# A decoder block's gated product and its broadcasts of 1/rms, from fp32 to fp32r in high and low parts

## The chip, the cores and the metric

The kernel runs on one core of one Trainium2 chip, in one launch. The metric is the device time of that core in microseconds. Three runs of the kernel before took 1047.62, 1047.27 and 1045.18 us; their median is 1047.27.

## The reference

One layer of a hybrid decoder block over 512 tokens of width 1024: a SwiGLU half-step, a mixer (sparse attention beside an S5 state-space layer), a second SwiGLU half-step, a gated per-layer embedding and a last RMSNorm. Everything is fp32. What the change touches is the norm and the S5 layer's gated product:

```python
def rmsnorm(x, g):
    xf = x.astype(jnp.float32)
    y = xf * lax.rsqrt(jnp.mean(xf * xf, axis=-1, keepdims=True) + RMS_EPS)
    return (y * g.astype(jnp.float32)).astype(x.dtype)

# at the end of s5_mixer: y is (1, 512, 512), w_glu is (512, 512)
    y = jax.nn.gelu(y.reshape(B, L, S5_WIDTH))
    out = y * jax.nn.sigmoid(y @ w_glu.astype(f32) + b_glu.astype(f32))

def reference(...):
    h = x
    h = h + 0.5 * swiglu(rmsnorm(h, norm_ffn1), ffn1_w1, ffn1_w3, ffn1_w2)
    z = rmsnorm(h, norm_mix) @ w_in
    ...
    h = h + jnp.concatenate([o_nsa, o_s5], axis=-1) @ w_out
    h = h + 0.5 * swiglu(rmsnorm(h, norm_ffn2), ffn2_w1, ffn2_w3, ffn2_w2)
    gate = jax.nn.sigmoid(rmsnorm(h, norm_ple) @ w_ple_gate)
    h = h + gate * (p @ w_ple)
    return rmsnorm(h, norm_final)
```

## The kernel before

**Layout.** The residual `h` stays in SBUF transposed: eight tiles of 128 features by 512 tokens. Weights come from DRAM in units of 128x1024 fp32 (512 KB), one after another on ScalarE's DMA queue, into a ring of four buffers `raw`.

**Products in three parts.** Most products use the type fp32r, and keep the precision by splitting both operands. `split` casts a unit to a high part `hi` on ScalarE (line 164) and subtracts that from the unit on VectorE to get a low part `lo` (line 166); the ring has three pairs of hi and lo. `mm3` (line 173) then issues three products, high by high, high by low and low by high, into one PSUM bank. A few products are written in plain fp32 with a single `mm`; the profile shows each of these as two records.

**Broadcasts of 1/rms.** `rsqrt_steps` (line 277) sums squares with products against a column of `ones`, takes the power -1/2 on GpSimd with one Newton step on VectorE, and has the result `ri` as 128 tokens by `nb` columns, one column for each 128 tokens. To spread it over partitions it scales the identity matrix by each column (`dg`, line 296) and multiplies `ones` (128x128) with `dg` (128x512) in one fp32 product (line 299). With `nb` = 4 this happens four times: for the first norm (`Norm.finish`, called in the first half-step), for the mixer's (`s5_input`), for the second half-step's (`norm2`, around line 1429) and for the gate's (`ng.finish`, line 1515). In the mixer and for `norm2` the broadcast is pinned to its place in TensorE's order (`pin_last`). The last norm of all uses `nb` = 2 twice.

**The mixer's order.** Attention, the S5 layer, the projections and the first half of the output product are generators; the string `PLAN` (line 1590) lists by hand in which order their steps are written: `g` is the GLU (line 1174), `s` the S5 scan, `c` the compression, `t` and `x` scores, `V` values, `p` the loads of queries, `f` half of the output product. A scheduler then orders each engine's instructions from that written order with its own model of times, except where an instruction is pinned or told to follow another (`issue_after`). The GLU's first four steps apply gelu to the four tiles `yts` (128 channels by 512 tokens). Its next four each make one block: four fp32 products of raw weights with the tiles, then tanh on ScalarE, a product on VectorE, and the split of the result into `oh` and `ol`, which the output product reads. At `close` the S5 buffers are given back and the attention's pool `ap_` takes their place, with four buffers each of the tags `eh` and `el` for the values' steps.

Of the kernel before, what the change touches and what calls it, by code (L numbers as in the profile page):

```python
# [10 lines left out]
F32 = mybir.dt.float32  # L11
FR = mybir.dt.float32r
# [3 lines left out]
OP = mybir.AluOpType  # L16
# [3 lines left out]
SEQ = 512  # L20
# [56 lines left out]
def block_kernel(ctx: ExitStack, tc: tile.TileContext, a: dict, out: bass.AP):  # L77
    nc = tc.nc
    V, S, G, PE = nc.vector, nc.scalar, nc.gpsimd, nc.tensor
    PS = bass.MemoryType.PSUM  # L80

    pers = ctx.enter_context(tc.tile_pool(name="pers", bufs=1, side="right"))
# [9 lines left out]
    def bank(tag, shape=(128, 512), dt=F32):  # L92
        return psum.tile(list(shape), dt, tag=tag, name="ps_" + tag)
# [7 lines left out]
    def load_unit(i, q, parts=None):  # L101
        w = UNIT_W[i]
        raw = ring.tile([128, UNIT], F32, tag="raw", name="raw", bufs=4)
        src = a["wpack"][128 * UNIT_OFF[i]:128 * UNIT_OFF[i + 1]]
        raws[i] = raw
        if parts is None:
            loads[i] = q.dma_start(raw[:, :w], src.rearrange("(p c) -> p c", c=w))
            return None
        src = src.rearrange("(n p c) -> n p c", p=128, n=len(parts))
        return [lambda c=c, i=i: q.dma_start(raw[:, c], src[i]) for i, c in enumerate(parts)]  # L110
# [12 lines left out]
    ident = pers.tile([128, 128], F32, name="ident")  # L123
    nc.sync.dma_start(ident, a["ident"])
    identb = pers.tile([128, 128], BF, name="identb")
    G.tensor_copy(identb, ident)
    ones = pers.tile([128, 128], F32, name="ones")
    G.memset(ones, 1.0)

    pinned = tc.keep_in_program_order  # L130

    def mm(o, lhsT, rhs, start, stop, **kw):
        return PE.matmul(o, lhsT, rhs, start=start, stop=stop, **kw)  # L133
# [10 lines left out]
    def unit(raw_only=False, keep=None, q=nc.scalar, after=None, at=None):  # L144
        i = unit_i[0] if at is None else at
        if at is None:
            unit_i[0] += 1
        w = UNIT_W[i]
        if i not in raws:
            load_unit(i, q)  # L150
        raw = raws.pop(i)
        if raw_only:
            return raw
        return split(raw, (slice(0, w),), keep, after)
# [15 lines left out]
    def split(raw, parts=(slice(0, UNIT),), keep=None, after=None, kept=free):  # L170
        return list(split_parts(raw, parts, keep, after, kept))[-1]
# [8 lines left out]
    npool = ctx.enter_context(tc.tile_pool(name="npool", bufs=1, side="right"))  # L180
# [96 lines left out]
    def rsqrt_steps(parts, nb, pin=False, pin_last=False, beside=None):  # L277
        st = bank("D", (128, 4))[:, :nb] if isinstance(parts, list) else parts
        for b in range(nb if isinstance(parts, list) else 0):
            for i, t in enumerate(parts):  # L280
                p = mm(st[:, b:b + 1], t[:, b * 128:(b + 1) * 128], ones[:, 0:1], i == 0, i == len(parts) - 1)
                if pin and b + i == 0:
                    pinned(p)
        ms, ri, t = (npool.tile([128, 4], F32, tag=n, name=n, bufs=2)[:, :nb] for n in ("ms", "ri", "nt"))
        p = V.tensor_scalar(ms, st, 1.0 / D_MODEL, 1e-6, OP.mult, OP.add)
        if beside:
            pinned(p)
        G.tensor_tensor(ri, ms, negh[:, :nb], OP.pow)
        if beside:
            beside()  # L290
        V.tensor_tensor(t, ri, ri, OP.mult)
        V.scalar_tensor_tensor(t, t, -0.5, ms, OP.mult, OP.mult)
        V.scalar_tensor_tensor(ri, t, 1.5, ri, OP.add, OP.mult)
        dg = npool.tile([128, 4, 128], F32, tag="dg", name="dg")[:, :nb]
        for b in range(nb):
            V.tensor_scalar(dg[:, b, :], ident, ri[:, b:b + 1], None, OP.mult)
        yield
        pb = bank("D")[:, :nb * 128]
        p = mm(pb, ones, dg.rearrange("p b t -> p (b t)"), True, True)
        if pin_last:  # L300
            pinned(p)
        if beside:
            pb2 = bank("C")[:, :nb * 128]
            pinned(mm(pb2, ones, dg.rearrange("p b t -> p (b t)"), True, True))
            yield pb, pb2
        yield ri, pb
# [540 lines left out]
    def mixer(ctx):  # L847
# [45 lines left out]
        at = {}  # L893
# [26 lines left out]
        def gelu2(o, x, w, tag):  # L920

            t = tp.tile([128, SEQ], F32, tag=tag, name="gt")[:, :w]
            act(t, x, AF.Square)
            V.scalar_tensor_tensor(t, t, 1 / 0.044715, x, OP.add, OP.mult)
            act(t, t, AF.Tanh, scale=math.sqrt(2 / math.pi) * 0.044715)
            V.scalar_tensor_tensor(o, t, 1.0, x, OP.add, OP.mult)
# [34 lines left out]
        for i in range(2):  # L961
            raw = tp.tile([128, SEQ], F32, tag=f"r{i + 1}", name="rope")
# [63 lines left out]
        yts = []  # L1026
# [147 lines left out]
        def glu():  # L1174
            for m in range(4):
                yt = yts[m]
                gelu2(yt, yt, SEQ, GT[m % 2])
                yield
            for m in range(4):
                if m % 2 == 0:  # L1180
                    raw = unit(True, at=next(at["glu"]))
                o = bank("A")
                for k in range(4):
                    q = (m * 4 + k) % 8
                    mm(o, raw[:, q * 128:(q + 1) * 128], yts[k], k == 0, k == 3)
                sg = mp.tile([128, SEQ], F32, tag="ra", name="sg", bufs=2)

                act(sg, o, AF.Tanh, scale=0.25, bias=bglu[:, m:m + 1])
                V.scalar_tensor_tensor(sg, sg, 1.0, yts[m], OP.add, OP.mult)
                S.activation(oh[:, 4 + m], sg, AF.Copy, scale=0.25)  # L1190
                V.scalar_tensor_tensor(ol[:, 4 + m], sg, 0.25, oh[:, 4 + m].bitcast(F32), OP.mult, OP.subtract)
                yield
# [133 lines left out]
        def values(qb, env):  # L1326
# [3 lines left out]
            for g in range(2):  # L1330
# [40 lines left out]
                for par in range(2):  # L1371
# [9 lines left out]
                    v=v_gates(), s=s5_all(), c=cmp_all(), g=glu(), f=out_half(range(4, 8)))  # L1381
# [3 lines left out]
        for step in PLAN.split():  # L1385
            if step == "close":
                s5x.close()
                ap_ = ctx.enter_context(tc.tile_pool(name="att", bufs=2, reuse_waits="tile"))
# [41 lines left out]
    for m in range(KT):  # L1430
        if m % 4 == 0:
            wu = unit()
        o = bank("B")
        for k in range(2):
            q = (m * 2 + k) % 8
            sl = slice(q * 128, (q + 1) * 128)
# [15 lines left out]
    with tc.tile_pool(name="gate", bufs=2, reuse_waits="tile") as gp:  # L1452
# [59 lines left out]
        for m in range(KT - 3):  # L1512
            o = products(m, unit(), slice(0, SEQ))
# [5 lines left out]
        for i, wu in wl.items():  # L1519
            sq = gated(i, products(i, wu, c0), c0)  # L1520
# [29 lines left out]
        sq = gated(7, os[7], c1, pinned, {"gt": ends(E[1]), "h": ends(E[2])})  # L1550
# [4 lines left out]
        pb, pb1 = rsqrt_rows(st, 2, beside=ends(KT))  # L1555
# [32 lines left out]


PLAN = """u u u k s s u k k q s q s Q p3 s s s k s Q s t3 t3 s t3 z t3 s s t3 s p3 s z t3 t3 s s t3 t3 s g t3 g t3 g t3  # L1590
v t3 c v v c t3 v c c p2 t2 t3 t3 t2 p2 c c c t2 c c t2 t2 c v t2 t2 t2 t2 t2 t2 t2 t2 t2 g close p1 p1 p0 x3
p0 g t2 g t2 g g t1 t1 x2 f S2 t1 f t1 t1 f t1 t1 f f t0 t0 R2 f x1 t0 R3 V3 V3 V3 V3 V3 V3 V3 V3 V3 V3 V3 V3
V3 V3 V3 V3 x0 f V3 t1 V3 V3 V2 V2 V2 V2 V2 t0 V2 V2 V2 V2 V2 S0 V2 R1 R0 V2 V2 V2 V2 V1 V1 V1 V1 V1 V1 V1
V1 V1 V1 V1 V0 V0 V0 V0 V0 V0 V0 f"""
# [155 lines left out]
```

## Time and profile before

| | |
|---|---|
| median of three runs | 1047.27 us (1045.18 to 1047.62) |
| the profiled execution: its own time | 1044.96 us |
| its span, first to last instruction | 1043.2 us |
| mean granted TensorE clock | 0.999 |
| TensorE products busy | 1030.2 us in 6057 instructions |
| VectorE busy | 824.5 us |
| ScalarE busy | 501.9 us |
| GpSimd busy | 159.2 us |

The profile is of one execution. Its page gives the busy time of each engine, the chain of work that ended last, and groups of instructions by line, operation and tile. PE is TensorE's products, PEld its weight loads, DVE is VectorE, ACT ScalarE, POOL GpSimd, SP SyncE. A row of the chain reads: start in us, length in us, engine, output tile, line, number of instructions. A row of the timeline reads: start, length, engine, line, operation, output from inputs, shape, count, and in brackets the idle time before it with what ended it. A row of a table by stages reads: the window, its length, then for PE, PEld, DVE, ACT and POOL the busy time and count, then clock, share of the DMA engines in use, and GB/s. Nearly all products go through the helper at line 133, so they are told apart by their tiles. An f32 in a product's form stands for fp32r as well; the tiles tell which it is.

### The profile page before, as it was taken

To read this page: it belongs to the slowest core of one execution; us is meant where nothing else is said; L and a number is where in the kernel's file an instruction comes from. 1 tells how busy PE (TensorE), PEld (TensorE's weight loads), DVE (VectorE), ACT (ScalarE), POOL (GpSimd) and SP (SyncE) were. 2 spreads that over 40 slices of the span, in tenths; PEclk is the share of its full clock that TensorE was granted. 3 is DMA by queue.
4 is the path that set the end of the run, shared out by engine and by line. 5 is a ranking of instruction groups with operands and counts; after the bars stand their busy time and mean duration, and the time that the engine had idled before them with its cause. 6 is when DMAs were issued, how large, how long until landed. Compare 5 with 4: busy or idle time off the path is not lost.

```text
span 1043.2 us, 15725 instructions
## 1 busy us (share of the span) xinstructions
PE 1030.2 (99%) x6057; PEld 875.7 (84%) x6057; DVE 824.5 (79%) x1382; ACT 501.9 (48%) x868; POOL 159.2 (15%) x180
## 2 busy tenths in 40 slices
PE   9999999999999999999999999999999999999997
PEld 6888888889889888776586688998899899899886
DVE  6798468988989766896688887996598588687666
ACT  6322232535336542476768855653365245245452
POOL 0003948207870200100000000000000000000001
PEclk9999999999999999999999999999999999999999
DMA  7434325636354748766410013433233333333412
GB/s 266 142 87 134 98 88 169 229 121 127 120 135 149 231 118 230 216 193 183 158 41 21 21 61 123 135 107 122 85 98 122 101 102 101 101 102 101 141 61 81
DMA packets 52394, 131.00 MB, mean 126 GB/s; under 512 B 10784, under 2 KB 19072, under 8 KB 52320
## 3 DMA queue, kind: packets, MB, share of 16 engines
q10 hardware_dynamic: 26352, 90.77, 27.3%
q0 software_dynamic: 5872, 17.93, 6.9%
q1 hardware_dynamic: 20096, 21.31, 6.5%
q8 instruction: 47, 0.77, 0.3%
q14 instruction: 27, 0.22, 0.1%
HBM read 114.09 MB, written 15.73 MB: 124 GB/s over the span
## 4 chain that ended last, share of the span: by engine, by line
PE 84%; DVE 5%; DMA 3%; POOL 3%; ACT 2%; issue 2%; SPq 0%; DVEq 0%; ACTq 0%; POOLq 0%
PE ps_A L133 25%; PE ps_C L133 24%; PE ps_B L133 20%; PE ps_D L133 15%; POOL ft L721 1%; POOL bt L720 1%; DMA kf<-kd 1%; DVE lo L166 1%; ACT e L918 1%; DMA kd<-r 1%; DVE el L1360 0%; DMA qf<-qd 0%; DMA h<-in_xT 0%; POOL ft L719 0%; POOL seen L559 0%
## 5 line engine op out<-in xcount | busy, mean ns | idle before, releaser
L164 ACT CAST hi<-raw 128x1024 fp32r<-128x1024 f32 (+2 forms) x143 | 144.4, 1010 | 250.3 <-PE ps_C L133 96.8
L133 PE MATMUL ps_C<-hq,hi 128*128 128x512 f32 x704 | 217.5, 390 | 0.2
L166 DVE TENSOR_TENSOR lo<-raw,hi 128x1024 fp32r<-128x1024 f32 (+2 forms) x143 | 174.2, 1219 | 40.6 <-ACT hi L164 39.9
L133 PEld LDWEIGHTS ps_C<-hq,hi 128*128 128x128 f32 x704 | 130.9, 188 | 28.1 <-DVE h L526 1.3
L133 PE MATMUL ps_C<-hq,lo 128*128 128x512 f32 x352 | 136.9, 389 | 0.0
L133 PE MATMUL ps_A<-xh,hi 128*128 128x512 f32 (+1 forms) x352 | 124.9, 355 | 0.5 <-ACT hi L164 0.5
L133 PE MATMUL ps_A<-xl,hi 128*128 128x512 f32 (+1 forms) x352 | 124.0, 352 | 0.1
L133 PE MATMUL ps_A<-xh,lo 128*128 128x512 f32 (+1 forms) x352 | 122.5, 351 | 0.2 <-DVE lo L166 0.2
L164 ACT CAST hi<-s 128x1024 fp32r<-128x1024 f32 x56 | 58.9, 1052 | 107.0 <-PE ps_D L133 60.9
L166 DVE TENSOR_TENSOR lo<-s,hi 128x1024 fp32r<-128x1024 f32 x56 | 70.7, 1262 | 19.9 <-ACT hi L164 19.7
L133 PEld LDWEIGHTS ps_C<-hq,lo 128*128 128x128 f32 x352 | 66.1, 188 | 13.8
L133 PEld LDWEIGHTS ps_A<-xh,hi 128*128 128x128 f32 x352 | 66.6, 189 | 10.2 <-ACT hi L164 0.7
L133 PEld LDWEIGHTS ps_A<-xh,lo 128*128 128x128 f32 x352 | 66.7, 189 | 9.5 <-DVE lo L166 0.6
L133 PEld LDWEIGHTS ps_A<-xl,hi 128*128 128x128 f32 x352 | 66.5, 189 | 9.7 <-DVE xl L192 0.8
L526 DVE SCALAR_TENSOR_TENSOR h<-ps_C,h 128x512 f32<-128x512 f32 x64 | 43.9, 687 | 36.6 <-PE ps_C L133 36.5
L133 PE MATMUL ps_B<-sh,lo 128*128 128x256 f32 x224 | 63.1, 282 | 0.3 <-DVE lo L166 0.3
L133 PE MATMUL ps_D<-sl,hi 128*128 128x256 f32 x224 | 63.1, 282 | 0.0
L133 PE MATMUL ps_B<-sh,hi 128*128 128x256 f32 x224 | 63.0, 281 | 0.0
L133 PE MATMUL ps_B<-sl,hi 128*128 128x256 f32 x224 | 62.9, 281 | 0.0
L133 PE MATMUL ps_D<-sh,hi 128*128 128x256 f32 x224 | 62.8, 280 | 0.0
L133 PE MATMUL ps_B<-xh,hi 128*128 128x512 f32 (+1 forms) x168 | 62.8, 374 | 0.0
L133 PE MATMUL ps_D<-sh,lo 128*128 128x256 f32 x224 | 62.6, 280 | 0.0
(440 smaller groups left out, 2474.4 us busy)
## 6 DMA issues: line engine op xcount, KB each, us to landing
raw<-in_wpack ACTq DMA_DIRECT2D x168, 512.0 KB, 3.5
si<-s5i POOLq DMA_DIRECT2D x8, 512.0 KB, 5.3
so<-s5o POOLq DMA_DIRECT2D x8, 512.0 KB, 5.6
h<-in_xT SPq DMA_DIRECT2D x8, 256.0 KB, 4.5
s5i<-fs POOLq DMA_DIRECT2D x1, 2048.0 KB, 11.5
xraw<-in_xT SPq DMA_DIRECT2D x8, 256.0 KB, 3.8
s5o<-gt POOLq DMA_DIRECT2D x1, 2048.0 KB, 13.4
s5i<-tcs POOLq DMA_DIRECT2D x2, 1024.0 KB, 10.4
```

The costliest lines, as they stand in the source:

```text
L133: return PE.matmul(o, lhsT, rhs, start=start, stop=stop, **kw)
L164: p, q = S.copy(hi[:, c], raw[:, c]), None
L166: q = V.tensor_tensor(lo[:, c], raw[:, c], hi[:, c].bitcast(F32), OP.subtract)
L526: V.scalar_tensor_tensor(h[:, m, :], o[m], 0.5, h[:, m, :], OP.mult, OP.add)
L720: G.tensor_tensor(bt, b2[:, 1], bc(psn[:, e]), OP.mult)
L721: G.tensor_tensor(ft[:, :, s_, :], ft[:, :, s_, :], bt, OP.add)
L918: S.activation(*args, **kw)
```

## The change

The kernel after does three things. The four broadcasts with `nb` = 4 are made of two fp32r products: `ri` is rounded to fp32r (`rh`), the rest `t` is taken, and both scale the identity into a `dg` of their own, the second in the buffer `sq`. The tile `ones` is declared as fp32r, and read as fp32 elsewhere. The GLU's sixteen fp32 products become `mm3`: the tiles are split into `yh` and `yl` in a new step after the four gelu steps, in the buffers `eh` and `el`, and the two weight units are split like all others. In `PLAN` one `g` is added between the two steps `p1`, for the new step.

```diff
@@ -124,7 +124,8 @@
-    ones = pers.tile([128, 128], F32, name="ones")
+    onesr = pers.tile([128, 128], FR, name="ones")
+    ones = onesr.bitcast(F32)
     G.memset(ones, 1.0)
@@ -291,6 +292,24 @@
         V.scalar_tensor_tensor(ri, t, 1.5, ri, OP.add, OP.mult)
+        if nb == 4:
+            rh = npool.tile([128, 4], FR, tag="ms", name="rh", bufs=2)
+            V.tensor_copy(rh, ri)
+            V.tensor_tensor(t, ri, rh.bitcast(F32), OP.subtract)
+            parts = []
+            for n, r in (("dg", rh.bitcast(F32)), ("sq", t)):
+                dg = npool.tile([128, 4, 128], FR, tag=n, name="dg", bufs=1)
+                for b in range(nb):
+                    V.tensor_scalar(dg[:, b, :], ident, r[:, b:b + 1], None, OP.mult)
+                parts.append(dg.rearrange("p b t -> p (b t)"))
+            yield
+            pb = bank("D")
+            for i, dg in enumerate(parts):
+                p = mm(pb, onesr, dg, not i, i == 1)
+                if pin_last:
+                    pinned(p)
+            yield ri, pb
+            return
         dg = npool.tile([128, 4, 128], F32, tag="dg", name="dg")[:, :nb]
@@ -1176,13 +1195,21 @@
                 gelu2(yt, yt, SEQ, GT[m % 2])
                 yield
+            ys = []
+            for yt in yts:
+                yh, yl = (ap_.tile([128, SEQ], FR, tag=n, name="y", bufs=4) for n in ("eh", "el"))
+                S.copy(yh, yt)
+                V.tensor_tensor(yl, yt, yh.bitcast(F32), OP.subtract)
+                ys.append((yh, yl))
+            yield
             for m in range(4):
                 if m % 2 == 0:
-                    raw = unit(True, at=next(at["glu"]))
+                    wu = unit(at=next(at["glu"]))
                 o = bank("A")
                 for k in range(4):
                     q = (m * 4 + k) % 8
-                    mm(o, raw[:, q * 128:(q + 1) * 128], yts[k], k == 0, k == 3)
+                    sl = slice(q * 128, (q + 1) * 128)
+                    mm3(o, wu[0][:, sl], wu[1][:, sl], *ys[k], k == 0, k == 3)
                 sg = mp.tile([128, SEQ], F32, tag="ra", name="sg", bufs=2)
@@ -1588,7 +1615,7 @@
-v t3 c v v c t3 v c c p2 t2 t3 t3 t2 p2 c c c t2 c c t2 t2 c v t2 t2 t2 t2 t2 t2 t2 t2 t2 g close p1 p1 p0 x3
+v t3 c v v c t3 v c c p2 t2 t3 t3 t2 p2 c c c t2 c c t2 t2 c v t2 t2 t2 t2 t2 t2 t2 t2 t2 g close p1 g p1 p0 x3
```

## The prediction

> **What bounds the kernel now.** I read the page first, then the groups of TensorE instructions with shapes kept apart, then the chain of waits around the changed places, then the timeline at each of them.
>
> ```profile
> PE 1030.2 (99%) x6057; PEld 875.7 (84%) x6057; DVE 824.5 (79%) x1382; ACT 501.9 (48%) x868; POOL 159.2 (15%) x180
> PEclk9999999999999999999999999999999999999999
> PE 84%; DVE 5%; DMA 3%; POOL 3%; ACT 2%; issue 2%; SPq 0%; DVEq 0%; ACTq 0%; POOLq 0%
> L133 PE MATMUL ps_A<-yt,raw 128*128 128x512 f32 x32 | 14.6, 599 | 0.0
> L133 PE MATMUL ps_D<-dg,ones 128*128 128x512 f32 x8 | 4.1, 592 | 0.0
> ```
>
> TensorE is busy 99% of the span at a full granted clock, and holds 84% of the chain that ended last. Time taken from its queue should therefore come off the end, unless what replaces it makes TensorE wait. The two changed groups hold 14.6 and 4.1 us. There are two records to each fp32 product: 16 GLU products give 32 records and 4 broadcasts give 8. Busy times are modelled and overlap, so I take prices from the pace of the chain:
>
> ```profile
> by line: PE ps_A L133 72.2%; PE ps_B L133 18.5%; PE ps_C L133 6.8%; PE ps_D L133 1.7%; DVE cosr L1127 0.9%; PE ps_C L1152 0.4%; PE ps_D L1322 0.3%; issue 0.1%
> 497.31 3.49 PE ps_A L133 x8
> 500.80 0.42 PE ps_B L133 x3
> 501.87 3.49 PE ps_A L133 x8
> 505.77 3.49 PE ps_A L133 x8
> 1000.24 2.72 PE ps_B L133 x12
> 36.86 0.86 PE ps_D L133 x2
> 1002.96 0.86 PE ps_D L133 x2
> ```
>
> The first row covers 483 to 546 us: around the GLU the chain is TensorE alone but for 1%. One GLU block (four fp32 products) costs 3.49 us, or 0.87 a product. The row at 1000.24 is the gate's ordinary work of twelve fp32r products, also 128x512, in 2.72 us, or 0.227 each. One fp32 broadcast costs 0.86.
>
> **The change, part by part.**
>
> GLU products on TensorE: 16 fp32 products become 48 fp32r products. A block falls from 3.49 to 12 x 0.227 = 2.72. Four blocks gain 4 x 0.77 = 3.1 us. So three passes in place of one product is a gain of a quarter only, because one fp32 product lasts as long as 3.8 fp32r ones. The Trainium skill, page FP8 and Floating Point Precision, section TensorE Precision Notes, counts four passes through the array for true FP32; with 0.227 each that is 0.91 a product and a gain of 16 x 0.227 = 3.6 us, an estimate. The row's 0.87 decides here and gives the 3.1.
>
> GLU operands: eight new splits. Their prices stand in rows of the same shapes:
>
> ```profile
> L327 ACT CAST hq<-t 128x512 fp32r<-128x512 f32 x30 | 18.7, 622 | 13.3 <-DVE t L401 13.3
> L1360 DVE TENSOR_TENSOR el<-e,eh x48: 628/692/693, 548.6 to 604.3; 128x512 fp32r<-128x512 f32 x48
> L926 DVE SCALAR_TENSOR_TENSOR yt<-gt,yt x4: 692/692/693, 448.9 to 487.1; 128x512 f32<-128x512 f32 x4
> 490.00:500.00 10.00, 10.00 (x60) 5.67 (x59) 3.55 (x9) 4.26 (x11) 0.00 (x0) 1.00 0.92 332
> 500.00:510.00 10.00, 10.00 (x38) 4.82 (x36) 7.66 (x10) 7.89 (x18) 0.00 (x0) 1.00 0.60 180
> ```
>
> The four activations need 4 x 0.62 = 2.5 us of ScalarE and 4 x 0.69 = 2.8 of VectorE. The two weight units need 2 x 1.05 = 2.1 and 2 x 1.23 = 2.5 (rows below). Together that is 4.6 on ScalarE and 5.3 on VectorE. The last of the four yt starts at 487.1 and is ready 0.69 later, at 487.8. Between 490 and 500 VectorE (third busy column) works 3.55 of 10 us and ScalarE (fourth) 4.26, so 6.4 and 5.7 us are free there: the new work fits and I cost it at nothing. If that cover is gone, because the subtractions are put ahead of older work, the price is what TensorE waits for them, up to 2.8; the second rival takes that up.
>
> The first GLU block: before, TensorE read the loaded weights directly. Now they must be cast and subtracted first, and this is the one wait that the change adds on the path.
>
> ```profile
> 492.16 0.33 ACTq L107 DMA_DIRECT2D raw<-in_wpack  x1
> 493.02 0.34 ACTq L107 DMA_DIRECT2D raw<-in_wpack  x1
> 494.66 0.33 ACTq L107 DMA_DIRECT2D raw<-in_wpack  x1
> DMA to landing us min/median/max: 3.3/4.4/5.5
> 499.09 1.04 ACT L164 CAST hi<-raw 128x1024 fp32r<-128x1024 f32 x1 [0.52 <-DMA raw<-in_wpack]
> 500.16 1.23 DVE L166 TENSOR_TENSOR lo<-raw,hi 128x1024 fp32r<-128x1024 f32 x1 [1.64 <-ACT hi L164]
> 518.51 2.98 PE ps_A L133 x15
> ```
>
> These are weight loads, the first split after them, and the first block of the output half, the next user of split weights. The load at 494.66 lands 4.4 later, at 499.06, and the cast of the first output unit starts at 499.09, having waited for it. So the loads go in order, and those at 492.16 and 493.02 are the two GLU units. The first lands near 496.6, just ahead of its block at 497.31. With the change the cast ends near 497.6 and the subtraction near 498.9. The first two products of the block need only the high part; the third needs the low one. With nothing put in between, the block is late by 498.9 - 497.3 - 2 x 0.227 = 1.2 us; with the longest landing of 5.5 it is 2.3. With enough score products put ahead of it, it is nothing. Those are there (0.42 us at 500.80, more behind the next blocks), but they need free banks. I take 0.8, nearer to the row with the median landing, with 0 and 2.3 as ends. A queue's order costs something too: behind a cast at the head of ScalarE stand the exponentials that empty the score banks, and TensorE's fillers wait for these. It is already so at 499.09, where the wait was 0.52, and it is inside the 2.3. The second unit lands near 497.8 and is split long before the third block. Two of the three hi/lo slots go to the GLU units, so the second and third output units wait for GLU blocks two and four. Block four is over well before the output half begins at 518.51, and each unit serves two of its blocks: covered. The raw slots come free earlier than before, at the subtraction, and nothing in the chain waits for these loads, so I count no gain.
>
> The broadcasts of 1/rms: four times one fp32 product (0.86) becomes two fp32r products (0.45), a gain of 0.4 each. Before them VectorE gets a cast and a subtraction of 128x4 and four more 128x128 products.
>
> ```profile
> 32.82 0.88 DVE L296 TENSOR_SCALAR dg<-ident,ri 128x128 f32<-128x128 f32 x4
> 36.70 1.02 PE L133 MATMUL ps_D<-dg,ones 128*128 128x512 f32 x2
> 376.00 0.17 DVE L293 SCALAR_TENSOR_TENSOR ri<-nt,ri 128x4 f32<-128x4 f32 x1
> 376.20 0.88 DVE L296 TENSOR_SCALAR dg<-ident,ri 128x128 f32<-128x128 f32 x4
> 377.03 1.22 DVE L166 TENSOR_TENSOR lo<-raw,hi 128x1024 fp32r<-128x1024 f32 x1
> 378.28 1.02 PE L133 MATMUL ps_D<-dg,ones 128*128 128x512 f32 x2
> 634.50 0.88 DVE L296 TENSOR_SCALAR dg<-ident,ri 128x128 f32<-128x128 f32 x4
> 635.98 1.02 PE L133 MATMUL ps_D<-dg,ones 128*128 128x512 f32 x2
> 997.42 0.87 DVE L296 TENSOR_SCALAR dg<-ident,ri 128x128 f32<-128x128 f32 x4
> 1002.80 1.02 PE L133 MATMUL ps_D<-dg,ones 128*128 128x512 f32 x2
> L296 DVE TENSOR_SCALAR dg<-ident,ri x20: 277/282/288, 32.8 to 1035.6; 128x128 f32<-128x128 f32 x20
> ```
>
> Four products of 0.28 us take 0.88, so they start 0.20 apart; a 128x4 step also starts 0.20 after the one before it (376.00 to 376.20). The low half is thus ready 0.2 + 0.2 + 4 x 0.2 = 1.2 us later than dg was.
> - First norm: 33.70 becomes 34.90, TensorE comes at 36.70. Gain 0.4.
> - Mixer's norm: 377.08 becomes 378.28. TensorE needs the high half at 378.28 and the low half at 378.51. Just in time: gain 0.4, with 0.2 us to spare. The subtraction of weights at 377.03 moves back by 1.2 to end near 379.5. The broadcast is followed by six products of its own projection (1.4 us, to 380.1 with the shorter broadcast), and only the third of the next projection reads a new low part: covered.
> - Second norm: 635.38 becomes 636.58. The high product goes at 635.98, the low one waits from 636.21 to about 636.6 and ends its slot at 636.83, where the fp32 product ended it (635.98 + 0.86 = 636.84). These products are pinned in TensorE's order, so nothing passes them. Gain 0.
> - Gate's norm: 998.29 becomes 999.49, TensorE comes at 1002.80. Gain 0.4.
>
> That is 1.2 together. The trace has no tensor_scalar that writes fp32r. From below it is no shorter than the f32 one. From above I take 0.42 us (the 128x512 cast to fp32r on VectorE at line 1356, four times as long, has that mean):
>
> ```profile
> L1356 DVE CAST eh<-e 128x512 fp32r<-128x512 f32 x14 | 5.9, 423 | 0.6 <-ACT e L918 0.5
> ```
>
> I take 0.28, since that cast pays nothing visible for its output type. At 0.42, with starts 0.34 apart, eight of them end 1.1 later still, and the two tight places lose about 1 us each: an end of +2. VectorE: DVE Perf Modes in the Trainium skill (section The DRAIN you can't avoid) speaks against such chains of short instructions: the next one starts only when the pipe has emptied. By that the extra steps last 0.17 + 0.17 + 4 x 0.28 = 1.5 instead of 1.2, an estimate that would add 0.3 us at the second norm. The row of four in 0.88 us shows starts 0.20 apart, so I keep 1.2.
>
> The moved steps: the gated product gets one more step in the written order, ahead of its products. It issues no DMA of its own. On the queues of SP and POOL nothing of the change stands. The weight loads are the same two, from ScalarE's queue.
>
> **Sum.** -3.1 (products) -1.2 (broadcasts) +0.8 (first block late) = -3.5 us. The profiled execution took 1044.96 (span 1043.2), so 1041.5. It is 2.3 under the median of the three runs, 1047.27. On the median the forecast is 1043.8. Behind the GLU comes a stretch, 546 to 606, whose chain lies on ScalarE and VectorE too; it is entered from TensorE's chain, so it starts earlier and keeps its length.
>
> **Rivals.**
>
> First, the GLU gain is largely given back at its first block: no filler, longest landing, 2.3 in place of 0.8, and wide fp32r diagonals at the mixer's norm lose 1. Net -1.0: 1043.9 for the profiled execution, 1046.3 on the median, no change. For it: the weights land only 0.7 us before their block. Against it: score products for other query blocks stand in the queue.
>
> Second, and on the other side: VectorE becomes the bound of the mixer's middle.
>
> ```profile
> 470.00:480.00 10.00, 10.00 (x77) 8.49 (x75) 6.56 (x13) 8.63 (x21) 1.17 (x2) 1.00 0.51 118
> 480.00:490.00 10.00, 8.88 (x61) 5.90 (x61) 8.70 (x17) 7.43 (x19) 0.00 (x0) 1.00 0.52 165
> 482.60 0.58 DVE L1127 TENSOR_TENSOR cosr<-cst,pe 128x256 f32<-128x256 f32 x1 [0.30 <-DMA cst<-vcd]
> ```
>
> The yt are made from 448.9 to 487.1, so the first subtractions can run as soon as their buffers are free. If they and the rest go ahead of older VectorE work, above all of the row at 482.60, for which TensorE waits, VectorE sets the pace here: +5.3, the GLU gain does not count, the broadcasts keep -1.2. Net +4.1: 1049.1, or 1051.4 on the median. It decides when VectorE has under 5.3 us free up to 516; the rows show 3.4, 1.3, 6.4 and 2.3 for the four tens from 470, so it would need the new work to be bunched before 490.
>
> Third, the change does not do what it says: fp32r products whose weights are ones, or whose moving operand was just written, go slower than 0.29 each, and the GLU gains nothing (3.49 / 12 = 0.29). With -1.2 +0.8 that gives 1046.9 on the median. The twelve in 2.72 speak against it.
>
> **How the numbers follow.** About 0.3% (3.1 us) is what a measurement of this kernel can tell from no change, so "faster" begins at 1044.1, right beside the forecast of 1043.8. The likeliest case has 0.70, with a range of its own from -4.5 (block not late, second norm gaining a little) to -2.0, that is 1042.8 to 1045.3 on the median; 0.50 of it is faster, 0.20 the same. The first rival has 0.17 and the third 0.03, both the same. The second has 0.10, slower. The range reaches down to the lowest run shown (1045.18) less 4.5 and up past the first rival to 1048.3; it leaves the second out.
>
> **What would show it.** Right: four GLU blocks of twelve at about 2.7 us in the chain, the first starting between 497.3 and 499; two broadcast records in 0.45 at the first and last norm, about 0.8 with a gap at the second. Wrong: a wait of the GLU products for lo of over 2 us; the row of cosr at 482.60 later than now and behind new subtractions; diagonals in fp32r longer than 0.3 us.

## The result and the profile after

The changed kernel takes 1053.50 us (median of six runs, 1051.49 to 1056.17), the kernel before 1046.77 in the same comparison (six runs, 1045.18 to 1047.62). The ratio is 1.0069, with a 95% interval of 1.0057 to 1.0081: slower by 6.7 us, where 1043.8 was forecast and the range ended at 1048.3. The loss is small, but clear of noise.

The profiled execution of the changed kernel took 1056.17 us (span 1054.4). These are its busy times, granted clock and the share of the chain by engine, from the page:

```profile
PE 1032.7 (98%) x6073; PEld 881.0 (84%) x6073; DVE 832.6 (79%) x1412; ACT 504.5 (48%) x874; POOL 159.3 (15%) x180
PEclk9999999999999999989999999999999999999999
PE 79%; DVE 7%; DMA 4%; ACT 3%; POOL 3%; issue 3%; ACTq 0%; SPq 0%; DVEq 0%; POOLq 0%
```

TensorE's share of the chain fell from 84% to 79%. DMA, VectorE and ScalarE took it over. The chain of waits shows where. The first row below groups the stretch from 483 to 523 us; in the kernel before, that chain was TensorE alone but for 1%.

```profile
by line: DMA qf<-qd 27.5%; PE ps_A L134 19.9%; DMA raw<-in_wpack 13.3%; ACT QA L1265 6.1%; ACT y L1201 4.1%; issue 3.8%; ACT ps_B L937 3.6%; PE ps_C L134 3.2%; ACT gt L937 2.1%; ACT ps_C L937 1.9%; PE ps_D L134 1.8%; DVE y L1202 1.7%; DVE Q
483.95 1.65 ACT y L1201 x3
492.46 8.18 DMA qf<-qd
504.52 5.33 DMA raw<-in_wpack
512.42 3.02 PE ps_A L134 x12
480.00:520.00 40.00, 34.83 (x210) 24.12 (x209) 26.73 (x46) 27.11 (x62) 0.00 (x0) 1.00 0.66 190
```

Three things stand in these rows. The chain now runs through the new casts of y, through loads of queries (`qf`) of which one took 8.18 us, and through a weight load of 5.33. A block of products is shorter than before (twelve in 3.02, next to 3.49 for four in fp32). And the last row, a table by stage, has TensorE busy for 34.83 of the 40 us. In the kernel before the same window reads:

```profile
480.00:520.00 40.00, 38.88 (x206) 22.98 (x206) 27.08 (x53) 26.86 (x70) 0.00 (x0) 1.00 0.58 191
```

So TensorE idles 4.0 us more in this window alone, though the change takes work away from it. To see where the time goes over the whole span, I compare the start of the same TensorE instructions in two traces. The table gives how much later they start than in the kernel before, in us (single profiled executions; the experiments' labels are explained below). What counts is the step from one row to the next: in e6_pool and e7_splits32, whose code is the same as before up to the gated product, the products are 1.3 and 1.0 us late at 360 already, so a difference of about 1 us between two traces means nothing by itself.

| at, in the kernel before | what lies ahead of it | after | e1_bcast | e2_glu | e5_late | e8_tail |
|---|---|---|---|---|---|---|
| 370 | first half-step | +0.2 | +0.2 | | | |
| 390 | mixer's norm | +1.7 | +1.6 | | | |
| 478 | S5, projections | +6.3 | | +0.4 | +1.5 | +0.8 |
| 548 | gated product, scores | +8.3 | | +4.2 | +1.1 | +1.4 |
| 560 | start of the values | +10.9 | +1.9 | +6.7 | +3.3 | +0.4 |
| 1030 | gate, last norm | +11.4 | +2.5 | +6.7 | +3.1 | +0.2 |

Four places lose: the mixer's norm, the stretch 478 to 548, the stretch 548 to 560, and a little at the gate. The step from 2 to 6 between 440 and 478 in "after" is not in e2_glu; the execution profiled is the longest of its six, and the last section comes back to it. The +1.5 of e5_late at 478 is of the same kind: its products went from -0.2 at 440 to +1.7 at 450, ahead of all that e5_late changes, while its clock stood at 0.66 from 445 to 450.

### The profile page after: what moved, and what is told of

It reads as the page before. It is cut to its first block, busy times and chain, and to the rows that moved or that the text cites. A ratio compares the mean times of both kernels' runs of the same rounds, so it can differ in the third digit from the quotient of the medians.

```text
span 1054.4 us, 15785 instructions
## 1 busy us (share of the span) xinstructions
PE 1032.7 (98%) x6073; PEld 881.0 (84%) x6073; DVE 832.6 (79%) x1412; ACT 504.5 (48%) x874; POOL 159.3 (15%) x180
## 4 chain that ended last, share of the span: by engine, by line
PE 79%; DVE 7%; DMA 4%; ACT 3%; POOL 3%; issue 3%; ACTq 0%; SPq 0%; DVEq 0%; POOLq 0%
PE ps_C L134 23%; PE ps_A L134 22%; PE ps_B L134 18%; PE ps_D L134 15%; DVE lo L167 1%; POOL ft L740 1%; DMA qf<-qd 1%; DMA raw<-in_wpack 1%; DMA qd<-r 1%; DMA kf<-kd 1%; POOL bt L739 1%; ACT hi L165 1%; DMA kd<-r 1%; DVE s L361 0%; POOL ft L738 0%
```

## The experiments

All compare with the kernel before on the same chip, whose median in these comparisons was 1046.3 to 1046.5. Not all experiments ran on one chip, so where two of them are compared with each other, the ratios are the safer figure.

**The two parts alone.** e1_bcast has only the broadcasts changed, e2_glu only the gated product and `PLAN`.

> The broadcasts of 1/rms alone are changed; the gated product and the written order are those of before. Theory A, the mixer's norm: on VectorE a weight subtraction that waits for its cast has slipped between the rounding of 1/rms and the rest of it, so TensorE stands 1.5 us at the pinned broadcast, and all later transfers of the mixer start later and collide. It expects the stall again and 2 to 6 us more than before. Theory B, the GLU's operands: the new casts in ScalarE's queue hold back the score exponentials and the weights of the GLU land late. It expects that this kernel is 1 us faster than before to 0.5 us slower.

> The gated product alone is changed, with the extra step in the written order; all broadcasts stay fp32. Theory A expects 2 to 3 us less than before, since nothing stalls at the mixer's norm. Theory B expects 3 to 6 us more than before, with TensorE waiting between 480 and 520 us.

e1_bcast took 1048.18 (ratio 1.0016, 1.0007 to 1.0026), e2_glu 1052.62 (1.0053, 1.0038 to 1.0068). Both parts lose by themselves, and the gated product loses most: 6.1 us by the medians, 5.5 by the ratio. Theory A has the stall at the mixer's norm right, but not its size (2 to 6 us expected, 1.7 measured), and it fails on e2_glu. Theory B has e2_glu right and fails on e1_bcast. There are two separate losses.

**The mixer's norm.** Two kernels have the whole change but take away its loss there. e3_mix32 leaves the mixer's broadcast in fp32. e4_lo_after tells the subtraction of the third `u` unit's weights to follow the diagonals:

```diff
-                    V.tensor_scalar(dg[:, b, :], ident, r[:, b:b + 1], None, OP.mult)
+                    state["dg"] = V.tensor_scalar(dg[:, b, :], ident, r[:, b:b + 1], None, OP.mult)
...
-                out.append(proj("u", TU[m % 2], sides[m]))
+                out.append(proj("u", TU[m % 2], sides[m], state["dg"] if m == 2 else None))
```

> The whole change, but the mixer's broadcast of 1/rms stays fp32 with one diagonal. Theory A expects 1 to 4 us less than before. Theory B expects 2 to 5 us more than before, as the GLU part is there in full.

> The whole change, and on VectorE the weight subtraction of the third u unit is told to follow the diagonals of the mixer's norm. Theory A expects no stall at the pinned broadcast and, like the kernel with the fp32 broadcast there, 1 to 4 us less than before. Theory B expects 2 to 5 us more than before.

They took 1051.99 (1.0052, 1.0038 to 1.0066) and 1052.27 (1.0047, 1.0032 to 1.0061), some 1.2 to 1.5 less than the changed kernel by the medians. The intervals overlap with the changed kernel's, so the times alone don't show it; the traces do: at the broadcast TensorE loses 1.5 us in the changed kernel (+0.2 at 375, +1.7 at 385), nothing in e3_mix32, and gains 0.4 in e4_lo_after. Theory A's 1 to 4 us less than before fails for both kernels, since the gated product's loss is still there. e11_bfix is the same order with the broadcasts alone, so without the gated product.

> Only the broadcasts in fp32r, the gated product as before, and the third u unit's subtraction told to follow the diagonals. Theory A (the 1.7 us of e1_bcast are the subtraction that slipped in at the mixer's norm): the 0.4 us of the first norm are left, 1045.4 to 1046.5, TensorE's products of the second half-step within 0.5 us of the kernel before. Rival (the loss is the longer way to the diagonals itself, four more multiplications and a rest): 1047.2 to 1048.2, as e1_bcast.

It took 1046.06 (0.9995, 0.9983 to 1.0008): the 1.7 us of e1_bcast are gone (the two intervals just touch). The timeline of VectorE and of TensorE's two products, first in the changed kernel and then in e11_bfix, shows why:

```profile
376.42 0.17 DVE L297 CAST rh<-ri 128x4 fp32r<-128x4 f32 x1
377.59 1.23 DVE L167 TENSOR_TENSOR lo<-raw,hi 128x1024 fp32r<-128x1024 f32 x1 [1.00 <-ACT hi L165]
378.73 0.15 DVE L298 TENSOR_TENSOR nt<-ri,rh 128x4 f32<-128x4 f32 x1
378.81 0.87 DVE L303 TENSOR_SCALAR dg<-ident,rh 128x128 fp32r<-128x128 f32 x4
379.59 0.87 DVE L303 TENSOR_SCALAR dg<-ident,nt 128x128 fp32r<-128x128 f32 x4
379.82 0.47 PE L134 MATMUL ps_D<-dg,ones 128*128 128x512 f32 x1 [1.15 <-DVE dg L303]
380.51 0.50 PE L134 MATMUL ps_D<-dg,ones 128*128 128x512 f32 x1 [0.23 <-DVE dg L303]
```
```profile
376.58 0.16 DVE L300 TENSOR_TENSOR nt<-ri,rh 128x4 f32<-128x4 f32 x1
377.44 0.87 DVE L305 TENSOR_SCALAR dg<-ident,nt 128x128 fp32r<-128x128 f32 x4
378.45 0.62 PE L134 MATMUL ps_D<-dg,ones 128*128 128x512 f32 x2
```

In the changed kernel VectorE stands idle for 1.00 us behind the cast `rh`, because the next instruction in its queue is a weight subtraction that waits for ScalarE; then it runs that for 1.23, and only then the rest and the diagonals. The pinned products wait 1.15 and 0.23. With the order mended the diagonals end at 378.3 and TensorE finds both ready.

**What in the gated product costs.** Three kernels on the base of e2_glu. e5_late emits the casts and subtractions of y right ahead of the first block; e6_pool has the casts of y on GpSimd; e7_splits32 makes all the splits but keeps the fp32 products.

```diff
 # e5_late, PLAN
-... g close p1 g p1 p0 x3
-p0 g t2 g t2 g g t1 ...
+... g close p1 p1 p0 x3
+p0 g g t2 g t2 g g t1 ...
 # e6_pool
-                S.copy(yh, yt)
+                G.tensor_copy(yh, yt)
 # e7_splits32
-                    mm3(o, wu[0][:, sl], wu[1][:, sl], *ys[k], k == 0, k == 3)
+                    mm(o, raw[:, sl], yts[k], k == 0, k == 3)
```

> The gated product's part alone (broadcasts in fp32), but the casts and subtractions of y are emitted in the step of the first block, so that ScalarE's order has both pairs of query casts (QA, QB) ahead of the three y casts; in e2_glu the casts stood ahead of the second pair, the second pair of query loads was issued at 485.99 and 486.61 instead of 483.19 and 483.81, collided with three loads of weights and took 6.7 and 8.3 us instead of 3.1 and 2.8, and the weights of the product landed at 504.1 instead of 496.6. Theory B1 (the loss is this queue: y casts ahead of query casts on ScalarE): second pair of query loads issued by 484, first GLU weights landed by 498, time 1043.5 to 1047.5, that is 0.995 to 1.001 of before. Theory B2 (the loss is that a block of the product must now wait for a split weight, load plus cast plus subtraction, some 2.5 us after the landing): the place of the y casts does not matter, first block still 5 us late, 1050 to 1053.5. Theory B3 (the loss is ScalarE's and VectorE's work itself, 4 x 0.61 + 4 x 0.69 + 2 x 1.2 + 2 x 1.2 us in a stretch where they feed the scores): 1049 to 1053.

> The gated product's part alone (broadcasts in fp32), with the casts of y to fp32r on GpSimd instead of ScalarE; the subtractions stay on VectorE, weights are split as in e2_glu. B1: ScalarE's order is that of before up to the weights' casts, query loads at 483.2 and 483.8 again, 1043.5 to 1047.5. B2: still 1050 to 1053.5. B3: half of ScalarE's added work is gone, VectorE's is not: 1048 to 1052. If GpSimd's cast is over 2 us each, the fourth one (its input is the last) can hold the first block back by that much.

> Only the splits: y and the gated product's weights are cast and subtracted as in e2_glu, in the same places, but the products stay fp32 on the unsplit y and weights, four instead of twelve per block; the split tiles are not read. B1: the y casts stand ahead of the second pair of query casts as in e2_glu, so the whole loss stays and TensorE's gain of 3.1 us goes with it: 1053 to 1057. B2: a block no longer waits for the split, so the loss goes: 1046 to 1049. B3: 1053 to 1057, like B1; e5_late and e6_pool tell B1 and B3 apart.

e5_late took 1047.48 (1.0008, 0.9996 to 1.0019), e6_pool 1048.25 (1.0014, 1.0003 to 1.0025), e7_splits32 1051.62 (1.0046, 1.0029 to 1.0063). Theory B1 holds in the main, for 4.4 to 5.1 us by the medians: the place of the y casts and subtractions makes that difference, with the same work on the same engines in e5_late. e6_pool is 0.7 above B1's band and inside B3's (1048 to 1052), so by itself it leaves room for some cost of the work; e5_late, with all of that work, lies inside B1's band. e7_splits32 came out a little under its band, but on the side of B1 and B3; B2 falls, since no product there reads a split weight. It shows more: with fp32 products it is no slower than e2_glu, so that the 3.1 us of TensorE work were worth nothing there.

How the casts cost this much is read from e2_glu, first its queue order on ScalarE and VectorE and the load that follows, then the same in e5_late. `qf<-qd` are the loads of queries; the count and the median time to landing stand at the end of a row of issues.

```profile
478.11 1.65 ACT L1182 CAST y<-yt 128x512 fp32r<-128x512 f32 x3
479.66 0.63 ACT L1246 ACTIVATE QA<-qf 128x512 fp32r<-128x512 f32 x1
482.11 0.69 DVE L1183 TENSOR_TENSOR y<-yt,y 128x512 fp32r<-128x512 f32 x1
483.92 1.29 DVE L1183 TENSOR_TENSOR y<-yt,y 128x512 fp32r<-128x512 f32 x2
485.24 0.69 DVE L1248 SCALAR_TENSOR_TENSOR QA<-qf,QA 64x512 fp32r<-64x512 f32 x1
486.61 8.29 DMA qf<-qd
qf<-qd SPq DMA_DIRECT2D x2, 128.0 KB, 7.5
```
```profile
479.21 0.62 ACT L1246 ACTIVATE QA<-qf 128x512 fp32r<-128x512 f32 x1
480.25 1.65 ACT L1182 CAST y<-yt 128x512 fp32r<-128x512 f32 x3
482.69 1.29 DVE L1248 SCALAR_TENSOR_TENSOR QA<-qf,QA 64x512 fp32r<-64x512 f32 x2
485.29 1.28 DVE L1183 TENSOR_TENSOR y<-yt,y 128x512 fp32r<-128x512 f32 x2
qf<-qd SPq DMA_DIRECT2D x4, 128.0 KB, 2.7
```

In e2_glu the casts of y stand ahead of the second pair of query casts, and on VectorE three subtractions of y, and the row of `cosr`, ahead of the second subtraction of queries. That subtraction gives a `qf` buffer back, at 485.9 instead of 482.3 before (there both run at 481.01 in one group of 1.29). The loads that wait for the buffer go out at 486.0 and 486.6, in the midst of three weight loads of 512 KB each, and take 7.5 us instead of 2.8. Behind them stand, in order, the last query casts, the fourth cast of y, and the queue that issues the weights. In e5_late the queries go first, and the four query loads take 2.7 (median). In e6_pool, where only the casts have left ScalarE, the two subtractions of queries also run together (at 485.09, 1.29 us) and the four loads take 2.9. B1 names ScalarE's queue; the rows have the late step on VectorE. No run moves the subtractions alone, so which of the two queues sets the order stays open.

Two things hang on it. The weights land late: the product's first unit is cast at 499.21 in e2_glu, and its first block starts at 500.30, 3.2 later than before. (The load that e5_late's expectation has landing at 504.1 is the next one, the first unit of the output half; the product's own had landed by 499.21.) And the second block comes behind that next unit, though it doesn't read it: the unit's cast waits for its load at the head of ScalarE's queue, and behind it stand the exponentials that empty the score banks and the first block's tanh (`sg`). In the changed kernel TensorE waits 1.25 us for such an exponential and 0.19 for `sg`:

```profile
509.86 1.05 ACT L165 CAST hi<-raw 128x1024 fp32r<-128x1024 f32 x1 [1.35 <-DMA raw<-in_wpack]
512.42 0.73 PE L134 MATMUL ps_A<-y,hi 128*128 128x512 f32 x2 [0.19 <-ACT sg L937]
```

Part of the price is the clock. After these waits e2_glu's granted clock was 0.71 from 505 to 510, and its second block took 4.62 us where 2.80 is the pace in e5_late:

```profile
506.71 4.62 PE ps_A L133 x12
```

The listed clocks of all runs show that this is no accident of one execution: their mean is 0.9967 over e2_glu's six runs and 0.9960 over the changed kernel's six, but 0.9979 in e5_late, 0.9981 in e6_pool and 0.9981 in the kernel before (17 runs). Of 1050 us, 0.0012 to 0.0014 are 1.3 to 1.5 us, an estimate of the clock's share in the 4.4 to 5.1.

**The rest of it.** e5_late is at last level with the kernel before, but not under it, and its column in the table still rises by 2.2 between 548 and 560. e8_tail moves the steps that give the softmax weights of the last query blocks ahead by one step of scores; e9_hifirst lets the eight products with the weights' high part go first in a block.

```diff
 # e8_tail, on e5_late
-... g t2 g g t1 t1 x2 f S2 t1 f ...
+... g t2 g g t1 x2 S2 t1 f t1 f ...
 # e9_hifirst, on e5_late
-                for k in range(4):
-                    mm3(o, wu[0][:, sl], wu[1][:, sl], *ys[k], k == 0, k == 3)
+                for p in range(3):
+                    for k in range(4):
+                        mm(o, wu[p == 2][:, sl], ys[k][p == 1], p + k == 0, p == 2 and k == 3)
```

> e5_late (gated product alone, y casts behind the query casts; 1047.48) with one change further on: x2 and S2, the steps that give the softmax weights of the last two query blocks, stand one step of scores earlier in PLAN. In e5_late the two products on VectorE that write those weights into the queries (QB from ps_D) stand behind the third h addition and run at 547.87 and 549.01, in the kernel before at 542.53 and 543.68; between 548 and 556 e5_late lost 2.1 us. Theory C1 (this order is where they are lost): QB ahead of that addition, 1045.4 to 1046.7. Theory C2 (the stretch only carries on the lateness of the gated product, whatever the order): 1047 to 1048.

> e5_late with the twelve products of a block in another order: four with the weights' high part on y's high part, four with it on y's low part, the four with the weights' low part last. A block then needs the weights' subtraction 8 x 0.227 = 1.8 us after its first product and not 0.45 us after. In e5_late the weights landed at 499.05, the cast ran at 499.08, the subtraction at 500.16 and, for the second unit, at 502.56, and the first block took 3.82 us instead of 2.72. Theory D1 (TensorE waits for the split weights, above all for their low part): 1045.5 to 1046.8. Theory D2 (what is late is the load itself or y, the low part is covered): 1047 to 1048.

> The kernel before, with nothing but e8_tail's edit of PLAN (x2 and S2 one step of scores earlier). In the kernel before the QB products are not behind the third h addition, so C1 expects no gain: 1046 to 1047.5. If this edit gains time of itself, 1044.3 to 1045, then e8_tail's 2.0 us are not a loss of the change that was given back.

e8_tail took 1045.50 (0.9993, 0.9983 to 1.0002), inside C1's band and 2.0 us under e5_late by the medians, 1.6 by the ratios, whose intervals overlap a little. e9_hifirst took 1048.16 (1.0018, 1.0007 to 1.0029), no better than e5_late: D1 falls. e15_ctl, the same edit in the kernel before, took 1048.63 (1.0018, 1.0008 to 1.0028): there it loses, so that e8_tail's 2 us are no general gain of that edit. That loss is above C1's band (1046 to 1047.5), but its trace has it in the same place: the second QB product now runs behind the third `h` addition (547.18 there), and TensorE goes from 1.5 us late at 540 to 3.7 at 556. So in both programs it is the place of QB that costs some 2 us. VectorE's rows and the window, of the kernel before, of e5_late and of e8_tail, and the row of e15_ctl:

```profile
542.53 2.35 DVE L1323 TENSOR_TENSOR QB<-ps_D,sel 48x1024 fp32r<-48x1024 f32 x2
550.00:560.00 10.00, 9.76 (x40) 6.22 (x38) 9.11 (x27) 8.43 (x23) 0.00 (x0) 1.00 0.09 34
```
```profile
547.15 0.69 DVE L1217 TENSOR_TENSOR h<-h,ps_A 128x512 f32<-128x512 f32 x1 [1.42 <-PE ps_A L133]
547.87 2.35 DVE L1331 TENSOR_TENSOR QB<-ps_D,sel 48x1024 fp32r<-48x1024 f32 x2
550.00:560.00 10.00, 8.58 (x34) 5.35 (x33) 8.82 (x21) 8.03 (x21) 0.00 (x0) 1.00 0.19 52
```
```profile
544.48 2.35 DVE L1331 TENSOR_TENSOR QB<-ps_D,sel 48x1024 fp32r<-48x1024 f32 x2
550.00:560.00 10.00, 10.00 (x44) 7.22 (x43) 9.14 (x27) 8.16 (x21) 0.00 (x0) 1.00 0.16 52
```
```profile
548.23 1.22 DVE L1323 TENSOR_TENSOR QB<-ps_D,sel 48x1024 fp32r<-48x1024 f32 x1
```

In e5_late the scheduler, which orders each engine anew for the changed program, had put the two QB products behind an addition for which VectorE idles 1.42 us. The maxima, the exponentials and TensorE's first products of the values stand behind them. This loss lies 30 us behind the last block of the gated product.

**Where the gain of 3.1 us is.** e8_tail is 0.8 under the kernel before, not 3.1, and its interval includes no change. e12_ka leaves out the reading of the split weights: its products read a tile that has long been there, so it doesn't compute the layer; e13_gelu changes an order on ScalarE.

```diff
 # e12_ka, on e8_tail
-                    mm3(o, wu[0][:, sl], wu[1][:, sl], *ys[k], k == 0, k == 3)
+                    wk = KA.rearrange("p b t -> p (b t)")[:, sl]
+                    mm3(o, wk, wk, *ys[k], k == 0, k == 3)
 # e13_gelu, on e8_tail ("cgt" is the tanh of the compressed keys' gelu)
-                    wu = unit(at=next(at["glu"]))
+                    raw = unit(True, at=next(at["glu"]))
+                    with tc.issue_after(state["cgt"].ins):
+                        wu = split(raw)
```

> e8_tail, but the gated product's 48 products read a tile that is long there (the keys, KA) in place of the split weights; the weights are still loaded, cast and subtracted as before, only not read, so the output is not the reference's. Left open by e8_tail (1045.50, 0.8 us under the kernel before): where the rest of TensorE's 3.1 us went. In 480 to 520 us TensorE was busy 38.89 us before and 37.50 in e8_tail, 1.4 us more idle. Theory E1 (it waits there for the split weights: landing at 497.58, cast 1.06, subtraction 1.22, with scores' work between them): without that wait 1.2 to 2.3 us go, 1043.2 to 1044.3. Theory E2 (TensorE waits there for the compressed keys' own loads, the fourth y or the scores' exponentials, whatever the weights): 1045 to 1046.

> e8_tail, with the split of the gated product's weights told to follow the tanh of the compressed keys' gelu, so that ScalarE's order has both activations of that gelu ahead of the casts of the weights. From the last product of the compressed keys to ht it took 2.3 us before (496.18 to 498.52), 5.5 in e8_tail (497.13 to 502.63) and 5.0 in e12_ka; TensorE's in-order queue has the transposes of ht ahead of a block of the gated product. Theory F1 (the casts in ScalarE's queue, waiting for their loads, are where the rest of the gain goes): gelu back to 2.3 to 3 us, 1043.2 to 1044.6. Theory F2 (with the casts behind it the blocks come late instead, rival 1 of the prediction): 1045 to 1046.5.

e12_ka took 1046.92 (0.9997, 0.9983 to 1.0012) and e13_gelu 1046.50 (1.0001, 0.9992 to 1.0010). E1 falls: blocks that need no split weights are no earlier in the end. F1's band is missed too; e12_ka lies above both of its bands, which no run explains. The rows of ScalarE and VectorE around the gelu of the compressed keys, in the kernel before, in e8_tail and in e13_gelu, with TensorE's wait and its busy time in e13_gelu:

```profile
496.22 0.38 ACT L918 ACTIVATE gt<-ps_A 128x256 f32<-128x256 f32 x1 [1.26 <-PE ps_A L133]
498.11 0.41 DVE L926 SCALAR_TENSOR_TENSOR ht<-gt,ps_A 128x256 f32<-128x256 f32 x1
```
```profile
497.60 1.05 ACT L164 CAST hi<-raw 128x1024 fp32r<-128x1024 f32 x1 [1.50 <-DMA raw<-in_wpack]
498.55 0.38 ACT L918 ACTIVATE gt<-ps_A 128x256 f32<-128x256 f32 x1
502.22 0.41 DVE L926 SCALAR_TENSOR_TENSOR ht<-gt,ps_A 128x256 f32<-128x256 f32 x1
480.00:520.00 40.00, 37.50 (x227) 26.08 (x226) 31.21 (x57) 29.25 (x71) 0.00 (x0) 1.00 0.59 180
```
```profile
501.40 1.99 ACT L164 CAST hi<-raw 128x1024 fp32r<-128x1024 f32 x2
502.07 0.44 PE L1153 MATMUL ps_C<-ident,ht 128*128 128x128 f32 x2 [1.28 <-DVE ht L926]
502.76 1.17 PE L133 MATMUL ps_A<-y,hi 128*128 128x512 f32 x4
480.00:520.00 40.00, 36.78 (x230) 26.55 (x228) 30.09 (x55) 29.42 (x70) 0.00 (x0) 1.00 0.56 178
```

In e8_tail the cast of the first weights idles ScalarE for 1.50 us, and the gelu behind it takes from 498.55 to 502.63 instead of 496.22 to 498.52; TensorE has the transposes of `ht` in front of the second block. With the gelu first, it is done 2.6 us after its input again, but now the transposes stand in front of the first block, which starts at 502.76, where it started at 497.14 before; 2.5 us of this the trace had at 478 already, 3.1 are new. As TensorE's order changed with it, e13_gelu is no clean test of F1. Either way TensorE idles in this window: 2.5 us in e8_tail and 3.2 in e13_gelu, next to 1.1 before. ScalarE and VectorE work 2 to 4 us more in it than before (29.25 and 31.21, next to 26.86 and 27.08). One or the other comes late, and at least part of the work that TensorE no longer has turns into waiting. The wait moves from version to version: in e8_tail it is 0.16 us for the weights' high part, 0.53 for their low part and 0.37 for a score bank, in e12_ka 0.63 for a load and 0.83 for `ht`, in e13_gelu 0.52 for a load and 1.28 for `ht`. Which single wait would have to go for the 3.1 us to come out stays open.

**Everything mended.** e10_all is the whole change with the four mends; e14_all2 adds the order of e13_gelu.

> The whole change (broadcasts and gated product) with all four mends: the third u unit's subtraction behind the diagonals (e4_lo_after), the y casts behind the query casts (e5_late), x2 and S2 earlier (e8_tail), the high products first (e9_hifirst). If C1 and D1 hold and the parts add up: e5_late's 1047.48 less 0.4 for the first norm, 1 to 2 for the order of QB and 0.7 to 1.5 for the order of the products, that is 1043.6 to 1045.4, at last near the 1043.8 that was predicted for the change. If C2 and D2 hold: 1046.5 to 1047.5.

> e10_all (the whole change with the four mends, 1045.09) with the gelu's order of e13_gelu too. F1: 1042.8 to 1044.2, the predicted 1043.8 within it. F2: 1044.8 to 1046.

e10_all took 1045.09 (0.9989, 0.9978 to 1.0000), e14_all2 1047.89 (1.0004, 0.9994 to 1.0014), above both of its bands. e10_all is inside the band of C1 and D1 although D1 had fallen, so that it doesn't confirm the sum behind that band. So the best version of the change is 1.2 us under the kernel before, at the edge of what this measurement can tell, and some 8 under the change as it was made.

## Why the prediction was wrong, step by step

- **GLU products, -3.1.** Nearly right as a size: where nothing comes between, twelve took 2.80 us in the chain of e5_late and 2.83 in that of e8_tail, next to 3.49 before and 2.72 forecast. The failure is that the chain was taken as TensorE's for good. Even in e8_tail, with the order mended, TensorE idles 1.4 us more between 480 and 520 than before, and only 0.8 of the 3.1 come out; e7_splits32, which keeps the fp32 products, is no slower than e2_glu.
- **GLU operands, 0.** This is the step that failed, for 4 to 5 us. "The new work fits" was read from the free time between 490 and 500. Three of the four y casts and subtractions were not done there. They became ready early and were put between 478 and 486, though VectorE had 8.70 of 10 us busy from 480 to 490 in the kernel before. The second rival has this place and this side; its price, 1051.4, is 2.1 short of the result, and that it comes so near is luck, as it was worked out for VectorE as the bound. It named the row of `cosr` as the older work at risk. That row hardly moved (482.93 in e2_glu next to 482.60). The victim was a subtraction that frees a load buffer, and the price came from the load that then met the weights, from what stood behind it in the queues, and from the clock that fell in the waits.
- **The first GLU block, +0.8, with 2.3 as the upper end.** Right only where the operands are in good order: in e8_tail the block starts at 498.70, before at 497.14, and 0.8 of these 1.6 us were there at 478. In the changed kernel it starts at 506.04, 8.9 later, of which 6.3 were there at 478: 2.6, above the end. And the term stopped at this block. The second starts at 512.42 in the changed kernel, 501.70 before, 10.7 later: the cast of the output half's first unit, waiting for its load, holds up the exponentials and the first block's tanh. That was not in the sum. The wait for the low part that the prediction named as the sign, over 2 us, was 0.53.
- **First norm, -0.4.** Right: TensorE is 0.4 earlier behind it in every kernel with the broadcasts. The two records don't follow each other, though: they start 0.70 apart, with two other products between them.
- **Mixer's norm, -0.4 "with 0.2 us to spare".** Wrong, and +1.5 instead. The subtraction of 377.03 did not move back. It went ahead, into the gap of one short instruction that the new cast opened, and took 1.00 of idling with it. With the order held (e11_bfix) the -0.4 is there.
- **Second norm, 0.** Right: the two records span 1.01 us, as the fp32 pair did (1.02).
- **Gate's norm, -0.4.** Right at the place (0.3 to 0.4 earlier at 1010), but between 1010 and 1030 the changed kernel, e1_bcast, e10_all and e11_bfix lose 0.9 each, and e2_glu and e8_tail, without the broadcasts, nothing. Before, TensorE entered the last column sums from its own chain; in e11_bfix they wait for VectorE:

```profile
1023.53 1.44 PE ps_A L133 x12
1024.97 0.80 PE ps_D L133 x8
```
```profile
1025.02 0.34 DVE accf L1517
1025.49 1.04 PE ps_D L134 x8
```

  No run takes this apart.
- **fp32r diagonals, 0.28.** Right: four in 0.87, the same as in f32. The Trainium skill, page VectorE: DVE Perf Modes, section The DRAIN you can't avoid, has in general each instruction wait for the pipe to empty, and adds that one that is not held starts earlier; the trace has that second case, with the starts 0.2 us apart again.
- **Not in the sum at all:** that the scheduler orders some 70 us anew, from the y casts at 478 down to the QB products at 547. The prediction took the order of everything that it didn't name as given. That cost 2.0 to 2.6 us.

## What to carry to other kernels

Work that is put on an engine with free time costs nothing only in the place where the time is free: ask when its inputs are ready and what stands behind it in the queue then, and above all which buffers that frees and which transfers wait for them. A short new instruction in a chain is a gap into which the scheduler can put a long one. And a saving on TensorE counts only as long as the chain stays TensorE's after the saving's own operands have been made.

## What the runs showed of the hardware

Transfers that collide hold each other up: a 128 KB load of queries took 2.8 us in the kernel before, ahead of the weight loads, and 8.18 in the changed kernel and 8.29 in e2_glu with three weight loads of 512 KB issued within 1 us of it.

The granted clock fell after short waits. In the profiled execution of the changed kernel TensorE was busy for 3.54 of 5 us from 450, with no single idle gap over 1.46 us, and then ran 5 us at half clock:

```profile
450.00:455.00 5.00, 3.54 (x34) 2.78 (x30) 4.02 (x6) 4.49 (x9) 0.76 (x1) 0.92 0.52 157
455.00:460.00 5.00, 5.00 (x16) 3.93 (x15) 4.86 (x9) 3.53 (x8) 0.00 (x0) 0.50 0.33 92
460.00:465.00 5.00, 5.00 (x32) 3.81 (x31) 4.84 (x12) 2.76 (x6) 0.75 (x1) 0.90 0.49 142
```

That is 5 x (0.08 + 0.50 + 0.10) = 3.4 us of TensorE time, an estimate. In the profiled execution of e5_late the clock was 0.66 from 445 to 450, after a gap of 1.36 us, in e2_glu 0.71 from 505 to 510, after one of 1.29, in e7_splits32 0.66 from 510 to 515, after one of 2.46. The busy share alone doesn't decide: in e2_glu TensorE was busy for 1.47 of 3.4 us from 498.2 and the clock stayed at 1.00 up to 505, then for 1.92 of 3.4 us from 503.7, and it fell. What does decide the runs don't show. The Trainium skill, page TensorE: Matmul & The Clock Gate, section HAM oscillation, gives as the rule that TensorE must not idle for more than some 3.4 us; here the clock fell after gaps of less than half that. The next section of that page of the Trainium skill, A second HAM failure mode: psum-queue depth-cycling, tells of a clock that goes to and fro when TensorE idles briefly and often between groups of products; the drops after 1.29 to 1.46 us agree with it.
